# Shared values and forget logits: five runs of 512, 512, 512, 264 and 264 columns in place of 512 and four of 388

## The chip, the cores and the metric

The kernel runs on one core of one Trainium2 chip. The metric is the time of one execution in microseconds on that core; lower is better. It is a median of three runs. A profile of a further execution shows which engine did what and when. The engines named in it are PE (TensorE, matrix products; PEld is its weight load), DVE (VectorE), ACT (ScalarE), POOL (GpSimd) and SP (SyncE, which here only starts transfers).

## What is computed

A two-layer decoder trunk on a sequence of 512 tokens, width 2048, in float32. Layer 0 is differential attention. After it, the residual stream is projected once into keys, values and forget-gate logits that layer 1 shares; layer 1 is forgetting attention that reads them. The part that matters here is the shared projection:

```python
def shared_kv(x, c_act, w_mod_kv, b_mod_kv, w_kv, b_f):
    ...
    hk = x * (1.0 + scale[:, None]) + shift[:, None]
    kvf = hk @ w_kv
    k, v, zf = jnp.split(kvf, [B_WIDTH, 2 * B_WIDTH], axis=-1)
    ...
    log_f = jax.nn.log_sigmoid(zf.astype(jnp.float32) + b_f.astype(jnp.float32))
    F = jnp.cumsum(log_f, axis=1)
    return k, v, F
```

`w_kv` has 2048 rows and 4112 columns: 2048 for the keys, 2048 for the values, and 16 for the forget logits, one for each head. Values and logits lie side by side, so together they are one product of 512 x 2048 by 2048 x 2064.

## The kernel before, in words

**Products.** Every float32 operand of a large product is split into two parts, a high one (`hi`, rounded) and a low one (`lo`, what is left). One block of a product is three matmuls: high by high, high by low, low by high (`products`, L199 to L203). Blocks are 128 deep: 2048 rows are 16 depth blocks.

**Weight stream.** `WeightStream` (L63) brings the weights in. A `Job` is a run of columns of one weight matrix; it is cut into 8 sub-steps of two depth blocks each. A sub-step is loaded into a stage tile `wst` of 128 x 2 x 512 elements (L88, four of them) by a transfer that SP starts (L59), copied by ACT into `whi` (L106, three of them), and DVE subtracts to get `wlo` (L107, three). Only the job's width of the tile is used. `get` (L132) casts two sub-steps ahead of the one that PE multiplies; `advance` (L127) starts loads three sub-steps further on.

**Groups.** `group` (L338) does one job: four sums in the four PSUM banks `acc`, one for each block of 128 tokens. For each of the 8 sub-steps and each bank it issues a burst of six matmuls (two depth blocks, three products). In the natural form, which the values use, a 128 x 128 block of the hidden state is the stationary operand and the weights are the moving one, so a matmul is as wide as the job. In the last sub-step each bank is emptied by `evac`. For each burst `tick` may issue a step of a background stream, by the count that `bg` gives.

**Background.** During this stage the background stream computes the second layer's modulation (`mod_stream`, L389): 192 blocks of 128 x 512 of `w_mod[1]`, 256 KB each, loaded by SP (L402) and summed on DVE (L426). Blocks 50 to 105 use tiles `msk` from the shared pool of 16 tiles (tag `K`) and are loaded up to seven ahead; the others use three tiles `ms` and are loaded two ahead.

**The shared projection.** The jobs of the values and logits are `vj` (L303, L304): one of 512 columns, then four of 388. The first is multiplied in an order of its own while the hidden state is still being built (L1412 to L1433). Four calls of `group` do the other four, each with one background step for every second burst (L1434, L1435). `evac_v` (L1356) copies a bank into a tile `vt` on ACT (L1360) and stores it to `v_dram` by a transfer that ACT starts (L1362). The last job holds the 16 logit columns at its end; `evac_v` keeps their tiles, and `forget_logits` (L1375) turns them on PE at the fourth burst that issues a background step in the first key group. Then the four key groups `kj` follow (512 columns each, background steps on three bursts of four), and layer 1.

**Order.** The first stage of the kernel runs by orders written out as strings. In all that follows the framework orders each engine's instructions and places the waits when it compiles, from its own estimate of when inputs are there; `keep_in_program_order` pins some DVE steps.

```python
    for g in range(1, 5):
        group(vj[g], True, evac_v(g), bg=lambda k: k % 2)
    pieces.extend([None] * 3 + [forget_logits, None, forget_sums] + [None] * 8 + [columns_of_f])
```

Of the kernel before, what the change touches and what calls it, by code (L numbers as in the profile page):

```python
# [137 lines left out]
def tile_yoco(  # L138
# [161 lines left out]
    phases = PHASES  # L300
    kj = [Job(kv_w, [(512 * g, 512)]) for g in range(4)]

    vcols = [0] + [512 + 388 * g for g in range(4)]  # L303
    vj = [Job(kv_w, [(2048 + col, 388 if col else 512)]) for col in vcols]  # L304
    bj = [Job(b_w_in, [(256 * p, 256), (2048 + 256 * p, 256)]) for p in range(8)]
    oA = [(f, Job(a_w_out, [(512 * f, 512)]), (0, 1, 2, 3)) for f in range(4)]
    oB = [(f, Job(b_w_out, [(512 * f, 512)]), (0, 1, 2, 3)) for f in range(4)]
# [1409 lines left out]
```

## Time and profile before

| what | value |
|---|---|
| median of 3 runs | 1940.69 us (1940.21 to 1940.83) |
| the profiled execution, its own time | 1940.17 us |
| span of its records | 1938.4 us |
| mean granted TensorE clock | 0.998 |
| first matmul of 388 columns starts | 1020.72 us |
| last matmul of 388 columns starts | 1162.32 us |
| matmuls of 388 columns recorded | 768 (3 x 256) |

The span counts from the first to the last instruction record; the execution's own time is 1.8 us longer. Times within the trace are counted from the start of the span. In a timeline row the first number is the start, the second the length of one instruction. The length of a matmul is the time that one takes from end to end; matmuls overlap, so what PE pays for one is the distance from its start to the start of the next.

### The profile page before, as it was taken

What the parts mean: (1) busy time and instruction counts of PE and PEld (TensorE: products, weight loads), DVE (VectorE), ACT (ScalarE), POOL (GpSimd) and SP (SyncE); (2) the same over time, 40 slices, a digit from 0 to 9 for tenths busy, and PEclk for the clock granted to TensorE, in tenths of its full rate; (3) what the DMA queues carried; (4) which work ended last, traced back from release to release, by engine and by line L of the source; (5) the groups of instructions that cost most, each with busy time, mean ns of one, the idle gap of its engine ahead of it and who ended that gap; (6) DMA issues with size and microseconds to landing.
All of it is one profiled execution on the core that took longest, in us unless ns stands there. A gap on an engine that the chain in (4) does not pass through costs nothing.

```text
span 1938.4 us, 25779 instructions
## 1 busy us (share of the span) xinstructions
PE 1918.7 (99%) x8941; PEld 1616.2 (83%) x8941; DVE 1358.4 (70%) x2546; ACT 731.4 (38%) x1250; POOL 2.2 (0%) x10
## 2 busy tenths in 40 slices
PE   8999999999999999999999999999999999999997
PEld 7888888888888888888889998888888888888886
DVE  7884588777776768667675657777566666687657
ACT  3546344333333344521273222224343434353123
POOL 0000000000000000000000000000000000000000
PEclk9999999999999999999999999999999999999999
DMA  9983466675767675376557756774354555554622
GB/s 341 385 301 115 153 185 203 210 237 187 237 198 224 204 233 170 122 240 221 174 174 254 269 186 213 253 262 158 114 156 149 153 153 157 152 172 153 224 93 103
DMA packets 351630, 382.19 MB, mean 197 GB/s; under 512 B 77926, under 2 KB 260860, under 8 KB 350732
## 3 DMA queue, kind: packets, MB, share of 16 engines
q1 hardware_dynamic: 348620, 376.35, 60.4%
q10 hardware_dynamic: 2880, 4.20, 0.6%
q8 instruction: 70, 1.15, 0.2%
q14 instruction: 60, 0.49, 0.1%
HBM read 348.65 MB, written 31.80 MB: 196 GB/s over the span
## 4 chain that ended last, share of the span: by engine, by line
PE 80%; DVE 2%; DMA 0%; issue 0%; ACT 0%; DVEq 0%
PE acc L201 25%; PE acc L202 25%; PE acc L203 25%; PE o L201 1%; PE o L202 1%; PE o L203 1%; PE sc L203 1%; PE sc L202 1%; PE sc L201 1%; DMA wst<-in_kv_w_dram 0%; DVE wlo L107 0%; PE sc L1299 0%; DVE ztmp L1207 0%; PE sc L209 0%; PE sc L208 0%
## 5 line engine op out<-in xcount | busy, mean ns | idle before, releaser
L106 ACT CAST whi<-wst 128x1024 fp32r<-128x1024 f32 (+2 forms) x298 | 303.3, 1018 | 642.9 <-PE acc L203 342.6
L107 DVE TENSOR_TENSOR wlo<-wst,whi 128x1024 fp32r<-128x1024 f32 (+2 forms) x298 | 351.2, 1179 | 246.2 <-ACT whi L106 240.8
L201 PE MATMUL acc<-hh,whi 128*128 128x512 f32 x1184 | 463.5, 391 | 0.0
L202 PE MATMUL acc<-hl,whi 128*128 128x512 f32 x1184 | 461.8, 390 | 0.0
L203 PE MATMUL acc<-hh,wlo 128*128 128x512 f32 x1184 | 460.9, 390 | 0.0
L201 PE MATMUL acc<-whi,hh 128*128 128x512 f32 (+1 forms) x1168 | 444.4, 380 | 0.0
L202 PE MATMUL acc<-wlo,hh 128*128 128x512 f32 (+1 forms) x1168 | 442.2, 379 | 0.0
L203 PE MATMUL acc<-whi,hl 128*128 128x512 f32 (+1 forms) x1168 | 441.9, 378 | 0.0
L426 DVE SCALAR_TENSOR_TENSOR macc<-ms,cact,macc 128x512 f32<-128x512 f32 x307 | 228.7, 745 | 62.7 <-DMA ms<-in_w_mod_dram 44.1
L203 PEld LDWEIGHTS acc<-hh,wlo 128*128 128x128 f32 x1184 | 222.3, 188 | 47.9
L201 PEld LDWEIGHTS acc<-hh,whi 128*128 128x128 f32 x1184 | 222.4, 188 | 43.5 <-issue 0.6
L202 PEld LDWEIGHTS acc<-hl,whi 128*128 128x128 f32 x1184 | 222.5, 188 | 41.9
L203 PEld LDWEIGHTS acc<-whi,hl 128*128 128x128 f32 x1168 | 219.2, 188 | 36.5 <-DVE hl L1293 0.2
L201 PEld LDWEIGHTS acc<-whi,hh 128*128 128x128 f32 x1168 | 219.2, 188 | 34.6 <-DVE ztmp L1207 0.4
L202 PEld LDWEIGHTS acc<-wlo,hh 128*128 128x128 f32 x1168 | 219.3, 188 | 33.7 <-DVE wlo L107 0.2
L607 DVE SCALAR_TENSOR_TENSOR sacc<-sms,cact,sacc 128x512 f32<-128x512 f32 (+1 forms) x123 | 87.5, 711 | 6.7 <-DMA sms<-in_w_mod_dram 3.5
L893 ACT ACTIVATE e<-e,mn 128x128 f32<-128x128 f32 (+3 forms) x64 | 36.0, 563 | 116.7 <-DVE mn L889 109.7
L1522 ACT ACTIVATE eb<-eb,mnb 128x128 f32<-128x128 f32 (+1 forms) x64 | 36.0, 562 | 83.5 <-DVE mnb L1519 82.6
L125 DVE TENSOR_TENSOR wlo<-wst,whi 128x768 fp32r<-128x768 f32 (+1 forms) x32 | 34.8, 1088 | 17.6 <-ACT whi L118 9.0
L709 PE MATMUL acc<-whi,hh 128*128 128x512 f32 x128 | 46.4, 394 | 0.0
L709 PE MATMUL acc<-whi,hl 128*128 128x512 f32 x128 | 45.9, 394 | 0.0
L889 DVE CUSTOM_DVE_ANT_0 e<-sc,bias 128x256 f32<-128x256 f32 (+2 forms) x48 | 26.4, 551 | 27.0 <-PE sc L203 26.9
(280 smaller groups left out, 1996.5 us busy)
## 6 DMA issues: line engine op xcount, KB each, us to landing
wst<-in_a_w_in_dram SPq DMA_DIRECT2D x240, 256.0 KB, 3.8
ms<-in_w_mod_dram SPq DMA_DIRECT2D x136, 256.0 KB, 3.9
ms<-in_kv_w_mod_dram SPq DMA_DIRECT2D x64, 512.0 KB, 3.7
wst<-in_b_w_in_dram SPq DMA_DIRECT2D x128, 256.0 KB, 2.8
sms<-in_w_mod_dram SPq DMA_DIRECT2D x56, 512.0 KB, 7.7
wst<-in_kv_w_dram SPq DMA_DIRECT2D x40, 512.0 KB, 4.2
ms<-in_w_mod_dram SPq DMA_DIRECT2D x32, 512.0 KB, 4.2
wst<-in_a_w_out_dram SPq DMA_DIRECT2D x32, 512.0 KB, 4.2
```

Of the source, the lines that this page charges most:

```text
L106: self.nc.scalar.copy(hi[:, :, :w], st[:, :, :w])
L107: self.nc.vector.tensor_tensor(lo[:, :, :w], st[:, :, :w], hi[:, :, :w].bitcast(F32), op=ALU.subtract)
L125: self.nc.vector.tensor_tensor(lo[:, :, :w], st[:, :, :w], hi[:, :, :w].bitcast(F32), op=ALU.subtract)
L201: PE.matmul(dst, lhs[0], rhs[0], start=start, stop=False)
L202: PE.matmul(dst, lhs[0], rhs[1], start=False, stop=False)
L203: PE.matmul(dst, lhs[1], rhs[0], start=False, stop=stop)
L426: ins = V.scalar_tensor_tensor(acc, w, cact[:, kt : kt + 1], acc, op0=ALU.mult, op1=ALU.add)
L607: V.scalar_tensor_tensor(acc, w, sc, acc, op0=ALU.mult, op1=ALU.add)
L709: PE.matmul(bank[n, bk], l, r, start=start, stop=stop, skip_group_check=True)
L889: V.tensor_tensor_reduce(out=e[:, :w], in0=sc[:, :w], in1=bias, scale=-1.0, scalar=3.0e38, op0=ALU.add, op1=ALU.min, accum_out=mn,)
L893: S.activation(e[:, :w], e[:, :w], AF.Exp, bias=mn, scale=-1.0, accum_out=rs)
L1522: S.activation(e[:, :w], e[:, :w], AF.Exp, bias=mn, scale=-1.0, accum_out=rs)
```

## The change

```diff
-    vcols = [0] + [512 + 388 * g for g in range(4)]
-    vj = [Job(kv_w, [(2048 + col, 388 if col else 512)]) for col in vcols]
+    vcols = [0, 512, 1024, 1536, 1800]
+    vj = [Job(kv_w, [(2048 + col, 512 if col < 1536 else 264)]) for col in vcols]
```

The 2064 columns are cut at other places. The first run stays as it is. The second and third become 512 wide, the fourth and fifth 264. The last run holds 248 value columns and the 16 logits, where it held 372 and 16. The number of groups, sub-steps, matmuls, casts, subtractions, loads, stores and background steps stays the same; what changes is how wide they are.

## The prediction

> **What bounds the kernel now.** I read the page's engine table, its slices and its chain first.
>
> ```profile
> span 1938.4 us, 25779 instructions
> PE 1918.7 (99%) x8941; PEld 1616.2 (83%) x8941; DVE 1358.4 (70%) x2546; ACT 731.4 (38%) x1250; POOL 2.2 (0%) x10
> ...
> PE   8999999999999999999999999999999999999997
> ...
> PEclk9999999999999999999999999999999999999999
> ...
> PE 80%; DVE 2%; DMA 0%; issue 0%; ACT 0%; DVEq 0%
> ```
>
> PE is busy in every slice at its full clock, and the chain that ends last is PE. A busy PE need not be at its peak, so next came the stage that the change touches: a table by windows, and the longest wait in it.
>
> ```profile
> core 0: us, PE busy (x) PEld busy (x) DVE busy (x) ACT busy (x) POOL busy (x), PEclk, DMA share, GB/s
> 1020.00:1057.00 37.00, 37.00 (x202) 35.54 (x202) 21.46 (x33) 11.37 (x17) 0.00 (x0) 1.00 0.79 275
> 1057.00:1092.00 35.00, 35.00 (x200) 35.00 (x199) 21.11 (x28) 9.18 (x14) 0.00 (x0) 1.00 0.70 235
> ...
> 1127.00:1163.00 36.00, 36.00 (x205) 35.91 (x204) 21.49 (x28) 9.95 (x15) 0.00 (x0) 1.00 0.67 216
> ```
>
> ```profile
> ACT whi L106 <- PE acc L203: 83.7, 26, 3.4
> ```
>
> From 1020 to 1163 us PE is never idle; DVE works 60% of the time (21.11 of 35.00 us) and ACT 26%. The longest wait runs from ACT to PE: ACT stands 83.7 us in 26 waits because PE still reads the `whi` buffer that the next weights need. Weights are ready early. So the stage lasts as long as PE needs to stream its matmuls, and the first price of the change is the distance from the start of one matmul to the start of the next.
>
> **The price of a matmul by its width.** Three cuts of the timeline of PE: the first and last of 176 matmuls of 388 columns in a row, of 19 of 512, and of six of 256 (from the attention of layer 1, which also loads new weights before each).
>
> ```profile
> 1055.01 0.33 PE L201 MATMUL acc<-whi,hh 128*128 128x388 f32 x1
> ...
> 1085.92 0.34 PE L202 MATMUL acc<-wlo,hh 128*128 128x388 f32 x1
> ```
>
> ```profile
> 1024.20 0.39 PE L203 MATMUL acc<-whi,hl 128*128 128x512 f32 x1
> ...
> 1028.28 0.39 PE L203 MATMUL acc<-whi,hl 128*128 128x512 f32 x1
> ```
>
> ```profile
> 1414.14 0.28 PE L201 MATMUL o<-pTh,vbh 128*128 128x256 f32 x1
> ...
> 1414.74 0.28 PE L203 MATMUL o<-pTh,vbl 128*128 128x256 f32 x1
> ```
>
> 388 columns: 30.91 us over 175 distances is 176.6 ns. 512: 4.08 us over 18 is 226.7 ns. 256: 0.60 us over 5 is 120.0 ns. The line through 256 and 512 rises 106.7 ns in 256 columns, 0.417 ns a column. It puts 388 at 175.0 ns, so the old width lies 1.6 ns above it, and 264 at 120.0 + 8 x 0.417 = 123.3 ns.
>
> **The change part by part: PE.** A group has 8 sub-steps x 4 banks x 6 = 192 matmuls. Four groups of 388 become two of 512 and two of 264, which is 384 pairs. A pair of 388 costs 353.2 ns; the pair 512 and 264 costs 226.7 + 123.3 = 350.0 ns. The gain is 3.2 ns x 384 = 1.2 us. No row shows 264 itself. From below its bound is the row of 256, 120.0 ns: a gain of 2.5 us. If 264 lies above the line as 388 does, it is 124.9 ns and the gain 0.6 us. The nearest wider row is 388; if 264 cost as much, 176.6 ns, the pair would cost 403.3 ns and the change would lose 50.1 x 384 = 19.2 us. I take 123.3, since the row of 256 is eight columns away and that of 388 is 124. The change breaks even at 126.5 ns.
>
> **ACT and DVE.** These rows are the groups of 1055 to 1163 us, shapes kept apart, and the evacuation copies of the whole kernel.
>
> ```profile
> L426 DVE SCALAR_TENSOR_TENSOR macc<-msk,cact,macc 128x512 f32<-128x512 f32 x48 | 35.9, 749 | 0.9
> L107 DVE TENSOR_TENSOR wlo<-wst,whi 128x776 fp32r<-128x776 f32 x23 | 22.2, 967 | 37.4 <-ACT whi L106 34.1 <-DMA wst<-in_kv_w_dram 1.8 <-DMA v_dram<-vt 1.4
> L106 ACT CAST whi<-wst 128x776 fp32r<-128x776 f32 x23 | 19.4, 844 | 67.2 <-PE acc L203 60.8 <-DMA msk<-in_w_mod_dram 6.4
> ...
> L107 DVE TENSOR_TENSOR wlo<-wst,whi 128x1024 fp32r<-128x1024 f32 x2 | 2.5, 1226 | 3.6 <-ACT whi L106 3.6
> L456 DVE STREAM_TRANSPOSE mturn<-macc 128x512 f32<-128x512 f32 x3 | 2.1, 712 | 0.1
> L106 ACT CAST whi<-wst 128x1024 fp32r<-128x1024 f32 x2 | 2.1, 1054 | 6.6 <-PE acc L203 6.6
> ```
>
> ```profile
> L1360 ACT COPY vt<-acc x20: 483/486/590, 1019.6 to 1162.7; 128x388 f32<-128x388 f32 x16, 128x512 f32<-128x512 f32 x4
> L1362 ACTq DMA_DIRECT2D v_dram<-vt x20: 326/326/417, 1020.2 to 1163.2; - x20
> ```
>
> The cast of 776 elements takes 844 ns and that of 1024 takes 1054, 0.85 ns an element, so 528 elements take some 634 ns. The subtraction falls from 967 to some 708 ns. A wide and a narrow sub-step together cost what two old ones did, on an engine with idle time: nothing on the path, as long as the narrow sub-steps are still supplied in time. They last 24 x 123.3 ns = 2.96 us, where the old ones lasted 4.24. In that time DVE has one subtraction and two background sums, 0.71 + 2 x 0.75 = 2.21 us, 75% of it; in every eighth a transpose and a reduction add 1.4 us. The cast of the sub-step two ahead starts when its buffer comes free, at the start of a sub-step; with the subtraction, and two sums in front of it, it is done 0.63 + 0.71 + 1.50 = 2.84 us later and needed after 5.92: 3.1 us to spare. In the last sub-steps the casts are already those of the 512-wide keys, 1.05 + 1.23 + 1.50 = 3.78 us, 2.1 us to spare. I cost both at nothing; if the cover were gone, each late sub-step would cost PE what it is late.
>
> Evacuation: a copy of 264 columns takes some 382 ns by the same kind of line, and ACT then spends 326 ns to issue the store, 0.71 us a bank, while PE finishes a bank every 6 x 123.3 = 740 ns. The next group comes back to the bank three bursts (2.2 us) later. It fits, with 1.5 us to spare; nothing.
>
> The entry into the stage: the first three sub-steps of the second run are cast while the hidden state is still being built, three times 0.21 us more on ACT and 0.26 on DVE. At most 0.8 us if PE waited for all of it. But the compiled order lets PE begin the second run before the first one ends; the rows are the first and the last of twelve such matmuls and the first of the old run behind them.
>
> ```profile
> 1020.72 0.34 PE L201 MATMUL acc<-whi,hh 128*128 128x388 f32 x1
> ...
> 1022.66 0.34 PE L203 MATMUL acc<-whi,hl 128*128 128x388 f32 x1
> 1022.84 0.39 PE L201 MATMUL acc<-whi,hh 128*128 128x512 f32 x1
> ```
>
> At 512 columns the twelve cover 12 x 226.7 ns, 2.7 us, instead of 2.1. I take nothing.
>
> **The transfers.** A narrow sub-step loads 264 KB of weights and two background blocks of 256 KB, 776 KB in 2.96 us, or 268 GB/s. For the two narrow groups, 47.4 us, I count at most: 16 x 264 KB, 248 KB more for each of the six loads that are already of the keys, 32 x 256 KB, and the stores of two groups (1024 and 528 KB), together 15,456 KB or 15.8 MB: 334 GB/s. Such a rate is shown elsewhere in this trace, in the window from 48.5 us, with its transfer table below it:
>
> ```profile
> 48.50:97.00 48.50, 48.50 (x237) 40.49 (x236) 43.13 (x61) 28.33 (x46) 0.00 (x0) 1.00 1.09 385
> ```
>
> ```profile
> DMA packets 18634, 18.65 MB, mean 385 GB/s; under 512 B 737, under 2 KB 17606, under 8 KB 18630
> ```
>
> 385 GB/s for 48.5 us, almost all in pieces under 2 KB, as rows of 264 columns (1056 bytes) are. The count of transfers, and so SP's and ACT's issue work, stays the same. Nothing, while the narrow rows reach the rate.
>
> **Sum.** The profiled execution took 1940.17 us with a span of 1938.4; less 1.2 us that is 1938.9 and 1937.2. The median of the runs is 0.5 us above that execution, so I predict 1940.7 - 1.2 = 1939.5 us. A measurement of this kernel can tell about 0.2%, 3.9 us, from no change; this gain is 0.06%.
>
> **Rivals.** *The weight load sets the pace.* Each matmul loads its own 128 x 128 weights, and in the window from 1057 us PEld is busy 35.00 of 35.00 us. If that were the bound, a matmul of 264 columns would take no less than one of 388, and the two narrow groups would lose 19.2 us: 1959.9 us. It begins to decide at 126.5 ns. The trace speaks against it: the six matmuls of 256 columns, with six weight loads, start 120.0 ns apart. For it speaks only that six are few, where 192 will come in a row.
>
> The Trainium skill, in Trainium Kernel Development and Optimization, section Performance Expectations, says that MFU and LDWEIGHTS busy percentage are the good measures of how near a kernel is to its roofline. By that rule this stage has no weight-load headroom left and the sum would be the loss just worked out. The trace does not agree: the loads overlap one another, so a row that is full at 176.6 ns still lets 120.0 ns through.
>
> *The transfers cannot feed the narrow groups*; this is the rival on the slow side that I hold likeliest. At the start of the two groups some 4 x 264 KB and 7 x 256 KB, 2.9 MB, may be on the chip already. The rest, 12.9 MB, fits in 47.4 us plus the 5.1 us at which a loss passes 0.2% if the rate is over 246 GB/s. At the 216 GB/s of the window from 1127 us it takes 59.7 us: 12.3 us late, less 1.2, or 1951.8 us. For it: no window of this stage shows more than 275 GB/s, and here loads share the queue with stores. Against it: those windows did not ask for more (of ACT's 67.2 us of idle time before the casts 6.4 are put down to a transfer), and 385 was reached where it was asked for.
>
> *Nothing gained*: 264 lies above the line like 388, or a newly compiled order costs a microsecond at the entry or the hand-over to the keys: 1940 to 1942 us. Against it: all spare times above. *Far faster*: only if 264 started under 116.3 ns apart, below the row of 256; nothing shows that.
>
> **How the numbers follow.** The forecast (a gain of 0.6 to 2.5 us) has 0.72, nothing gained 0.17, the transfers 0.06, the weight load 0.03, far faster 0.02. The forecast's range is 1938.2 to 1940.1; with the case of nothing gained it reaches 1942, and below I add 0.4 us for the spread of the runs: 1937.8 to 1942.0 holds 0.89 of the cases. To reach the two slow cases would stretch it by 10 us for less than a tenth. Faster by over 0.2%: 0.02; slower: 0.09; within: 0.89.
>
> **What would show it.** In the changed profile, matmuls of 264 columns start 123 ns apart (120 to 125), those of 512 still 227; the last value matmul starts 1.2 us earlier than 1162.3. ACT still waits for PE in the narrow groups, no wait of PE on `whi`, `wlo` or a bank appears, and DMA reaches 270 to 330 GB/s there. Wrong would be a distance above 126.5 ns, idle PE between 1113 and 1165 us, where the narrow groups and the hand-over will lie,, or a time outside 1937.8 to 1942.0.

## The result and the profile after

The changed kernel takes 1938.39 us, median of 22 runs (1937.7 to 1939.92), against 1940.79 for 22 runs of the kernel before: 2.4 us less, ratio 0.9987 with a 95% interval of 0.9982 to 0.9993. It is faster by 1.4 to 3.5 us. The forecast was 1.2 us faster, 1939.5. The result lies near the fast end of the 1938.2 to 1940.1 that the forecast's own gains allow, and inside the whole range, 1937.8 to 1942.0.

The page of the changed kernel, the lines that answer to those of before:

```profile
span 1936.4 us, 25779 instructions
PE 1915.8 (99%) x8941; PEld 1598.8 (83%) x8941; DVE 1359.3 (70%) x2546; ACT 730.8 (38%) x1250; POOL 2.2 (0%) x10
...
PE 81%; DVE 1%; issue 0%; DVEq 0%; ACT 0%
```

As many instructions, the same bound. DVE and ACT are as busy as before, and PE is 2.9 us less busy. The windows of the two narrow groups (columns as in the prediction's table by windows):

```profile
1114.00:1137.00 23.00, 23.00 (x193) 23.00 (x193) 17.97 (x27) 6.39 (x12) 0.00 (x0) 1.00 0.89 292
1137.00:1161.00 24.00, 24.00 (x199) 23.86 (x198) 19.09 (x27) 7.78 (x14) 0.00 (x0) 1.00 0.88 293
```

PE is never idle there, the clock is full, DVE works 78 to 80% of the time and the transfers run at 292 GB/s. The timeline of PE gives the price of a matmul: the first and the last of 193 of 264 columns in a row, and the first one of the keys behind them.

```profile
1136.98 0.28 PE L203 MATMUL acc<-whi,hl 128*128 128x264 f32 x1
...
1160.02 0.28 PE L203 MATMUL acc<-whi,hl 128*128 128x264 f32 x1
1160.14 0.39 PE L201 MATMUL acc<-hh,whi 128*128 128x512 f32 x1
```

23.04 us over 192 distances is 120.0 ns. The forecast took 123.3.

**A yardstick inside the trace.** Whole executions of one kernel differ by 2 us and more, so the experiments are read mainly on a stretch that holds just the changed groups: from the last transposes of the hidden state (L1299) to the transposes of the logits (L1378), on PE. First the kernel before, then the changed one.

```profile
1012.07 0.60 PE L1299 MATMUL sc<-ident,n 128*128 128x128 f32 x4
...
1167.98 0.60 PE L1378 MATMUL tr<-ident,vt 128*16 128x128 f32 x4
```

```profile
1012.49 0.60 PE L1299 MATMUL sc<-ident,n 128*128 128x128 f32 x4
...
1165.63 0.60 PE L1378 MATMUL tr<-ident,vt 128*16 128x128 f32 x4
```

155.91 us became 153.14: the stretch is 2.77 us shorter. The whole execution gained somewhat less in the median, 2.4 us. What lies ahead of the stretch took 1012.1 to 1013.5 us in the ten profiles of this document that have no sweep, and what lies behind it 770.4 to 771.2 us, so it varies by more than the difference. The two profiles of the kernel before are the shortest of the ten in both parts; a small loss outside the stretch is therefore not ruled out.

### The profile page after: what moved, and what is told of

Its sections match the earlier page's. It is cut to its first block, busy times and chain, and to the rows that moved or that the text cites. A ratio compares the mean times of both kernels' runs of the same rounds, so it can differ in the third digit from the quotient of the medians.

```text
span 1936.4 us, 25779 instructions
## 1 busy us (share of the span) xinstructions
PE 1915.8 (99%) x8941; PEld 1598.8 (83%) x8941; DVE 1359.3 (70%) x2546; ACT 730.8 (38%) x1250; POOL 2.2 (0%) x10
## 3 DMA queue, kind: packets, MB, share of 16 engines
q1 hardware_dynamic: 348620, 376.35, 60.7%
## 4 chain that ended last, share of the span: by engine, by line
PE 81%; DVE 1%; issue 0%; DVEq 0%; ACT 0%
PE acc L201 25%; PE acc L202 25%; PE acc L203 25%; PE o L201 1%; PE o L202 1%; PE o L203 1%; PE sc L203 1%; PE sc L202 1%; PE sc L201 1%; PE sc L1299 0%; DVE wlo L107 0%; PE sc L209 0%; PE sc L208 0%; DVE hl L1309 0%; DVE z L1682 0%
```

## The experiments

**Theory.** The gain is the spacing of matmuls and nothing else: a position (one matmul in each of the four groups) falls from 4 x 176.7 to 226.7 + 226.7 + 120.0 + 120.0 ns. **Rival.** Part of it comes from the entry, where the second run is now wider, or from the hand-over to the keys. Beside these stands the question why 264 columns cost 120.0 and not 123.3 ns.

### The price by width, measured by itself

Behind the changed kernel's last step (its outputs are unaffected) two tiles are copied from the result, and PE runs matmuls from them, a new weight load before each:

```python
    for c, n, k in runs:          # weight columns, moving columns, how many
        dst = acc_bank("sweep")
        for j in range(k):
            q = (j % (512 // c)) * c
            tc.keep_in_program_order(PE.matmul(dst[0:c, 0:n], stat[:, q : q + c], movg[:, 0:n], start=True, stop=True))
```

The first sweep goes from narrow to wide, 24 of each width, and then varies the weight columns.

> The changed kernel, with a sweep of matmuls added behind its end: first 48 of 512 columns to warm up, then 24 in a row of each of 31 widths from 128 to 512 columns with a new weight load of 128 columns each, then seven widths with weights of 64 and of 32 columns. Only the spacing of starts within each run is read, not the time. Theory F (a floor): a matmul that loads 128 weight columns cannot start sooner than 120.0 ns after the one before, whatever its width, and above some width near 270 columns the spacing rises by about 0.41 ns a column; then 248 to 264 columns all show 120 ns, and with 64 or 32 weight columns 256 and 264 columns fall below 120 and differ by some 3 ns. Rival S (steps): the cost of the moving columns rises in steps of several columns; then 256 and 264 share a step, further flat stretches show up between 272 and 512 columns, and the number of weight columns changes nothing. The old forecast's straight line would give 123.3 ns for 264 columns and 126.7 for 272.

The second goes from wide to narrow, 48 of each.

> The sweep again behind the changed kernel, from wide to narrow, 48 matmuls of each width, finer steps around 264, and five runs at the end that repeat widths. Only the spacing is read. If the spacing belongs to the width, each width repeats the first sweep within 1 ns: 264 at 120 to 121, 272 at 125, 388 at 176.5, 448 at 206.5, 512 at 226.5. If it belonged to the place in the sweep, to the length of a run or to what runs beside it, the departures from a straight line (264 some 3 ns below, 448 some 6 above) do not come back.

A row of the timeline that joins successive matmuls has the start of the first, the time to the end of the last, and the count; the spacing is that time less the length of one (0.28 us at 256 and 264 columns, 0.34 at 388, 0.39 at 512), over the count less one. Prices without a row here are means over the starts of all matmuls of a run. Each row below is cut from the middle of its run. The second sweep:

```profile
2230.68 10.59 PE L1702 MATMUL sweep<-movg,stat 128*128 128x512 f32 x46
```

```profile
2010.08 9.68 PE L1702 MATMUL sweep<-movg,stat 128*128 128x448 f32 x47
```

```profile
2055.54 8.29 PE L1702 MATMUL sweep<-movg,stat 128*128 128x388 f32 x46
```

```profile
2135.93 5.93 PE L1702 MATMUL sweep<-movg,stat 128*128 128x272 f32 x46
```

```profile
2159.86 5.68 PE L1702 MATMUL sweep<-movg,stat 128*128 128x264 f32 x46
```

```profile
2177.08 5.67 PE L1702 MATMUL sweep<-movg,stat 128*128 128x256 f32 x46
```

```profile
2199.12 5.19 PE L1702 MATMUL sweep<-movg,stat 128*128 128x128 f32 x45
```

That is 226.7 ns for 512 columns, 202.5 for 448, 176.7 for 388, 125.3 for 272, 120.0 for 264, 119.8 for 256 and 111.8 for 128. Between the last two, 192 and 240 columns took 111.3 and 111.9, and 248 took 115.0. The first sweep gave 226.7, 206.5, 176.6, 125.2, 121.0 and 119.2 for the same six widths from 512 down to 256: all within 1 ns but 448, which came back 4 ns lower. Of the other widths, 276 came back 2.5 ns higher. So the spacing belongs to the width to within a few ns, and it is a curve: flat at 111 to 112 ns up to 240 columns, 119 to 120 from 256 to 264, then 125 at 272 and about 0.44 ns a column up to 504 (226.6), with 512 no dearer than 504.

The single distances of a run are mostly not equal. They go through a short pattern that repeats, of 171 to 172 and 181 to 182 ns in turn at 388 columns, and the price is its mean. One width can settle into different patterns: at 448 columns nearly all distances were 206 and 207 ns in the first sweep, and 199 to 207 in the second. That is where the 4 ns come from.

And with fewer weight columns, from the first sweep:

```profile
2082.67 2.81 PE L1703 MATMUL sweep<-movg,stat 128*64 128x264 f32 x22
```

```profile
2107.68 2.81 PE L1703 MATMUL sweep<-movg,stat 128*32 128x264 f32 x22
```

```profile
2085.66 2.54 PE L1703 MATMUL sweep<-movg,stat 128*64 128x256 f32 x21
```

264 columns cost about 120 ns (120.2 from the starts) with 64 and with 32 weight columns. That takes away theory F as stated: if the 120 ns were a floor of the weight load, they would have come down. Nor are 120 ns a floor with 128 weight columns, where 248 columns cost 115.0 in both sweeps; what looks like a floor lies lower, at 111 to 112 ns. At 256 columns the price did come down, to 113 ns with 64 weight columns and 117 with 32, so the weight load may have a part in that row, though not one that grows with its columns. Steps (S) fit in part: 256 to 264 columns lie close together, and so do 376 and 384 (173.3 and 173.5 ns) and 504 to 512. But most widths in between rise without a step, and with 64 weight columns 256 and 388 columns cost 5.5 and 3 ns less than with 128, where S had no change. Neither theory had the curve.

### Half the change, two orders, other widths

Each of these kernels differs from the changed one only in the widths, for instance

```diff
-    vj = [Job(kv_w, [(2048 + col, 512 if col < 1536 else 264)]) for col in vcols]
+    vj = [Job(kv_w, [(2048 + col, w)]) for col, w in zip(vcols, [512, 512, 264, 388, 388])]
```

with `vcols` to match. One pair:

> Runs of 512, 512, 264, 388, 388 columns: half of the change. If the gain is the spacing alone (6.5 ns for each of 192 pairs), this is 1.25 us faster than before and 1.25 slower than the changed kernel: 1939.5 us. If part of the gain comes from the entry, where the second run is now 512 wide, that part (up to 1 us) is there already: 1938.5 to 1939.0 us.

The narrow runs first:

> Runs of 512, 264, 264, 512, 512 columns: the same widths as the changed kernel, the narrow ones first. If the gain is the spacing alone, the time is that of the changed kernel, 2.5 us below before: 1938.3 us. If the wide second run at the entry, or the wide run before it, gives part of the gain, the time is 0.5 to 2 us longer than the changed kernel's: 1939 to 1940.5 us; PE would then stand idle between 1000 and 1040 us.

Another pair of narrow widths:

> Runs of 512, 512, 512, 272, 256 columns. Theory F: if 272 columns lie on the floor of 120.0 ns too, the time is that of the changed kernel within 0.3 us; if the slope has begun, at most 192 x 6.7 ns = 1.3 us longer. Rival S: 272 columns would be on the next step and cost up to 1.3 us. The straight line has no loss here (264 + 264 and 272 + 256 cost the same), but puts both at 246.7 ns a pair.

The narrow runs in the middle:

> Runs of 512, 512, 264, 264, 512 columns: the widths of the changed kernel, the narrow ones in the middle, behind a wide second run. If the narrow-first kernel lost its time at the entry (PE waiting while the hidden state is finished, 0.9 us in its trace from 1020 to 1040 us), this one has no such loss and takes the changed kernel's time within 0.5 us. If what matters is the hand-over from the narrow runs to another wide run, or the distance of the narrow runs from the keys, it takes 0.7 us or more longer.

Widths in between:

> Runs of 512, 512, 448, 336, 256 columns, as many columns in as many matmuls. By the spacings of the first sweep (226.5, 206.5, 153.5 and 119.1 ns) the four groups cost 705.6 ns a matmul position against 693.9 for the changed kernel, 2.2 us more over 192 positions, so the gain over the kernel before is all but gone. By the straight line through 256 and 512 columns that the forecast used (226.7, 200.0, 153.3, 120.0) they cost 700.0, 1.2 us more than the changed kernel measured.

The changed kernel again, to compare with the last two:

> The changed kernel once more, as the common yardstick for the kernels of this call. Expected as before: 2.4 us below the kernel before, with 264 columns 120.0 ns apart.

And, for the entry alone, one pair behind a second run of 388, with the kernel before run again:

> Runs of 512, 388, 512, 264, 388 columns: the same widths as the one-pair kernel, but the second run is 388 wide as before. Read is the stretch from the last transpose of the hidden state (L1299) to the first transpose of the logits (L1378), which was 155.91 us before, 153.14 in the changed kernel and 154.41 in the one-pair kernel. By spacing alone one pair shortens it by 192 x 6.4 ns = 1.22 us. If a wide second run gives a further 0.3 us at the entry, this kernel lacks it: 154.7 us. If the 0.3 us has another cause (a slower stretch of the 388 runs, chance), it is 154.4 like the one-pair kernel.

> The kernel before once more, for how well the same stretch repeats between executions: 155.91 us within 0.05 if it can carry differences of 0.3 us, as the changed kernel's two profiles do (153.14 and 153.13).

The ends of the stretch in each, from the timelines of PE, in the order: one pair, narrow first, 272 and 256, middle, 448 and 336 and 256, 388 at the entry, changed again, before again.

```profile
1012.21 0.60 PE L1299 MATMUL sc<-ident,n 128*128 128x128 f32 x4
...
1166.62 0.60 PE L1378 MATMUL tr<-ident,vt 128*16 128x128 f32 x4
```

```profile
1013.01 0.60 PE L1299 MATMUL sc<-ident,n 128*128 128x128 f32 x4
...
1167.75 0.60 PE L1378 MATMUL tr<-ident,vt 128*16 128x128 f32 x4
```

```profile
1012.51 0.60 PE L1299 MATMUL sc<-ident,n 128*128 128x128 f32 x4
...
1166.63 0.60 PE L1378 MATMUL tr<-ident,vt 128*16 128x128 f32 x4
```

```profile
1012.21 0.60 PE L1299 MATMUL sc<-ident,n 128*128 128x128 f32 x4
...
1165.35 0.60 PE L1378 MATMUL tr<-ident,vt 128*16 128x128 f32 x4
```

```profile
1013.47 0.60 PE L1299 MATMUL sc<-ident,n 128*128 128x128 f32 x4
...
1168.37 0.60 PE L1378 MATMUL tr<-ident,vt 128*16 128x128 f32 x4
```

```profile
1013.09 0.60 PE L1299 MATMUL sc<-ident,n 128*128 128x128 f32 x4
...
1167.70 0.60 PE L1378 MATMUL tr<-ident,vt 128*16 128x128 f32 x4
```

```profile
1012.67 0.60 PE L1299 MATMUL sc<-ident,n 128*128 128x128 f32 x4
...
1165.80 0.60 PE L1378 MATMUL tr<-ident,vt 128*16 128x128 f32 x4
```

```profile
1012.18 0.60 PE L1299 MATMUL sc<-ident,n 128*128 128x128 f32 x4
...
1168.10 0.60 PE L1378 MATMUL tr<-ident,vt 128*16 128x128 f32 x4
```

In the table the gain is 155.91 less the stretch. "By spacing" is 192 times what a position saves by the second sweep's prices (336 columns: 153.4 ns); "left" is the rest. The times are medians of 11 runs, unless one run is said, with the ratio to runs of the kernel before taken alongside. Their median was 1941.21 us for the kernels with one pair, with the narrow runs first and with 272 and 256 columns, and 1941.18 for the other three.

| widths after the first 512 | stretch | gain | by spacing | left | median us | ratio (95%) |
|---|---|---|---|---|---|---|
| 388 388 388 388 (before, again) | 155.92 | 0.0 | 0 | 0.0 | 1940.38 (one run) | |
| 512 512 264 264 (changed, again) | 153.13 | 2.78 | 2.57 | 0.21 | 1939.34 | 0.9990 (0.9981 to 0.9999) |
| 512 264 264 512 | 153.14 | 2.77 | 2.57 | 0.20 | 1938.40 | 0.9985 (0.9976 to 0.9994) |
| 512 264 388 388 | 154.41 | 1.50 | 1.29 | 0.21 | 1939.59 | 0.9993 (0.9984 to 1.0001) |
| 388 512 264 388 | 154.61 | 1.30 | 1.29 | 0.01 | 1940.05 (one run) | |
| 512 512 272 256 | 154.12 | 1.79 | 1.59 | 0.20 | 1939.58 | 0.9990 (0.9981 to 0.9999) |
| 512 448 336 256 | 154.90 | 1.01 | 0.84 | 0.17 | 1940.43 | 0.9994 (0.9985 to 1.0003) |
| 264 264 512 512 | 154.74 | 1.17 | 2.57 | -1.40 | 1940.53 | 0.9995 (0.9986 to 1.0004) |

The stretch repeats to 0.01 us in the two profiles that each of the kernel before and the changed one has. Every kernel with a 512-wide second run gains what the spacing gives and 0.17 to 0.21 us more; the one whose second run is 388 wide gains what the spacing gives. So the spacing carries 2.57 of the 2.77 us, and the entry 0.20, less than the 0.3 that the expectation put there.

The widths in between test the curve. 272 and 256 columns made the stretch 0.98 us longer than 264 and 264, where the straight line had no loss. With 448, 336 and 256 columns the stretch was to be 2.2 us longer than the changed kernel's by the first sweep, and 1.2 by the straight line; it was 1.77 longer. In that kernel 448 columns start 202.7 ns apart, as in the second sweep, and not 206.5.

The hand-over to the keys does not show: with the narrow runs in the middle the stretch is the same. The median of that kernel is 0.94 us below the changed kernel's beside it. Nothing in the stretch explains that, and the changed kernel's own median was 1938.39 us in its 22 runs and 1939.34 here, so medians do not settle differences below 1 us.

Where the 0.20 us sit can be seen in the kernel before. These matmuls are the last of the first run, right behind the early ones of the second:

```profile
1023.30 0.39 PE L203 MATMUL acc<-whi,hl 128*128 128x512 f32 x1
1023.63 0.50 PE L201 MATMUL acc<-whi,hh 128*128 128x512 f32 x1
1023.97 0.40 PE L202 MATMUL acc<-wlo,hh 128*128 128x512 f32 x1
```

Two distances are 0.33 and 0.34 us where a 512 costs 0.227: 0.21 us lost. The waits of the same place name what PE waited for, first in the kernel before, then with the narrow runs first:

```profile
PEld acc L201 <- ACT hh L1292: 0.3, 1, 0.3
PEld acc L203 <- DVE hl L1293: 0.2, 1, 0.2
```

```profile
PEld acc L201 <- ACT hh L1292: 0.6, 2, 0.3
...
PEld acc L203 <- DVE hl L1293: 0.3, 2, 0.2
PEld acc L201 <- ACT vt L1360: 0.2, 1, 0.2
```

The last blocks of the hidden state are not finished when PE comes back to the first run. Twelve early matmuls of the second run cover that time: 12 x 176.7 ns were slightly too few, 12 x 226.7 suffice (the changed kernel has none of these waits), and with 12 x 120.0 the waits grow from 0.5 to 1.1 us. Against the kernels with a wide second run the narrow-first one lacks 1.6 us. Its trace shows three parts. The distances from 1020 to 1025 us are 0.90 us longer than the prices allow. Two more at 1030 us are together 0.23 us too long:

```profile
1030.07 0.28 PE L203 MATMUL acc<-whi,hl 128*128 128x264 f32 x1
1030.31 0.39 PE L201 MATMUL acc<-whi,hh 128*128 128x264 f32 x1
1030.54 0.28 PE L202 MATMUL acc<-wlo,hh 128*128 128x264 f32 x1
```

There PE's weight load waits 0.2 us for ACT, which empties a bank of the first run into `vt`. And of the 382 distances of 264 columns all but four long ones average 121.3 ns, 0.5 us in all: they repeat 116, 120, 121, 126 and 124 ns, the pattern of the first sweep at this width, where in the changed kernel nearly all are 120. What picks the pattern is not shown by any run here.

## Why the prediction was right, and where its size was off

- **The bound and the path.** Right, but for the entry. PE streams through the changed stage, and what changes is the distance between matmul starts. The last value matmul starts at 1160.02 where it started at 1162.32, 2.3 us earlier and not 1.2. That PE was "never idle" before was read from a busy row, 37.00 of 37.00 us; the 0.21 us of waiting at 1023 us lie in that row unseen, and show only in the distances between starts and in the waits of PEld.
- **The price of 264 columns.** The mis-sized term. The forecast drew a straight line through 256 and 512 and took 123.3 ns; the trace shows 120.0, the row of 256 itself, which the forecast had given as its lower bound with a gain of 2.5 us. The prices are not on a line: 388 already lay 1.6 ns above it, a sign that the line was not to be trusted, and the forecast used that sign only towards a smaller gain. With 120.0 for 123.3 the sum becomes 2.5 us by the forecast's own numbers for 388 and 512, 2.57 by the sweep's. That the median gained 2.4 us, so close to this, is partly luck: the stretch gained 2.77, and what lies ahead of and behind it varies by 1.4 and 0.8 us.
- **The entry.** Taken as nothing, from a possible loss of 0.8 us. It was a gain of 0.20: the cover by twelve wider matmuls, which the forecast named as its reason, was worth more than the longer casts may have cost; that cost was not measured by itself.
- **ACT, DVE and the evacuation.** Right. The narrow cast took 638 ns (634 estimated), the subtraction 707 (708), the copy 377 (382). PE waited for none of them in the narrow groups:

```profile
L107 DVE TENSOR_TENSOR wlo<-wst,whi 128x528 fp32r<-128x528 f32 x14 | 9.9, 707 | 7.8 <-ACT whi L106 6.4 <-DMA wst<-in_kv_w_dram 1.3
L106 ACT CAST whi<-wst 128x528 fp32r<-128x528 f32 x14 | 8.9, 638 | 26.2 <-PE acc L203 19.5 <-DMA msk<-in_w_mod_dram 4.5 <-DMA mod_dram<-mrow 2.2
L1360 ACT COPY vt<-acc 128x264 f32<-128x264 f32 x8 | 3.0, 377 | 2.3 <-PE acc L203 2.2
```

- **The transfers.** Right. 292 GB/s lie between the 268 and 334 of the working. The rival fell: the narrow groups asked for more than any window of this stage had shown before (275 GB/s) and got it. One argument for the rival was also mistaken: loads and stores do not share a queue. The page of the kernel before lists 376.35 MB in queue q1 and 4.20 MB in q10, which is the size of the 20 stores that ACT starts.
- **The weight load.** The rival fell. In the window from 1114 us PEld is busy 23.00 of 23.00 us, and its 193 matmuls still start 120 ns apart. A full row of weight loads says as little here as a full row of matmuls: it was full at 176.7 ns too. At 264 columns fewer weight columns do not lower the price by more than the two sweeps differ (120.2 ns against 121.0 and 120.0).

What stays open is why the price has this shape: why it hardly rises from 256 to 264 columns and not at all from 504 to 512, and climbs faster in between. The sweeps show that the shape repeats to within 4 ns, and that the number of weight columns does not set the price at 264; no run here tells what makes it, nor what picks the pattern of distances within a width.

## What to carry to other kernels

Where PE streams without idle time, cutting the same columns in the same number of runs can still gain, because the price of a matmul is not linear in its width: in this kernel two matmuls of 388 cost 353 ns, and one of 512 and one of 264 cost 347. Price each width from a row of that width, or measure it in a sweep behind the kernel's end, and treat a row that lies off the line as a warning about the line in both directions. And where a run serves as cover for work of another engine, its width is part of the cover: the same narrow runs at the entry lost 1.1 us of the 2.77 in waits.

## What the runs showed of the hardware that was not expected

In the sweep, matmuls with a new load of 128 weight columns start 111 to 112 ns apart at 128, 192 and 240 columns alike (111.8, 111.3, 111.9); the transposes of L1299, which also load 128 columns each time, start 108 ns apart (1012.07 to 1012.39 us for four). From 256 to 264 columns the price is 119 to 121 ns, with 128, 64 or 32 weight columns alike at 264. From 504 to 512 columns it does not rise (226.6 and 226.7 ns). The distances of one width repeat in patterns, and one width can take several: 448 columns cost 206.5 ns in one sweep and 202.5 in the other.
